# Opening products in another term order, later sample norm, two PSUM tiles for the last product, earlier sample gate

## The chip, the cores and the metric

One Trainium2 chip, one NeuronCore. The metric is the device time of one execution in microseconds (us). Engines are named as in the profile: PE is the matrix engine (PEld its weight loads), DVE the vector engine, ACT the scalar engine, POOL GpSimd, SP the engine that issues most DMAs.

## The reference, cut to what matters

One decoder layer over 1024 prompt rows and 8 sample rows of 1024 channels, all in float32:

```
xn = rmsnorm(h);  proj = xn @ w_in            # 1024 x 7168, split into u, v, z_a, x_b, z_b, g_a, g_b
y_a = gelu(u) * spatial_mix(layernorm(gelu(v))) * silu(z_a)
y_b = pooled(x_b) * silu(z_b)
m = sigmoid(g_a) * (y_a @ w_pa) + sigmoid(g_b) * (y_b @ w_pb)
h = h + rmsnorm(m @ w_out) * post_g
e = p @ w_ple
gate = sigmoid(rmsnorm(h) @ w_pg)
h = h + rmsnorm(gate * e) * ple_out_g
```

The prompt's result and the sample's result are both outputs, with some rows of v and of the pooling input.

## The kernel before, in words

Every large product is cut in seven by Strassen's scheme (P1 to P7), and each factor is split into a high and a low part (`split`, line 432: ACT writes the high part, DVE the difference), so that one product of 512 x 512 blocks is 3 matmuls for each of 4 blocks of the contraction: high x high, high x low, low x high. `product` (line 663) issues these 12 matmuls. The blocks of the normalised input are called B11, B21, B22 and T1 to T4; T1 to T4 are sums of the former that DVE makes in the opening.

No order is written out by hand for the middle of the kernel. The program is first recorded as operations (`Planner.take`, line 211), and a list scheduler (`Planner.order`, line 274) then gives each engine its fixed order by a time model: an operation starts not before its due time minus a lead, among those that could start the one with the earliest due time is taken (`rank`, line 305), and `PUSH` (line 32, through `pushed`, line 989) moves the due time of single kinds of operations: a positive number makes it earlier, a negative one later. All instructions are emitted by `play`, so every row of the profile names L374. At run time each engine works its order off strictly, waiting where an operand is not there. Most tiles live in 46 slots of SBUF that the scheduler hands out; PSUM has three regions of two banks (`region`) and two single banks (`bank`).

Four stages matter here.

- **Opening** (0 to about 70 us). `begin` (line 1726) issues the loads in a fixed order (`WE` and `LOADS` place the weights w_ple and the second v weights among the x tiles). Nine warming matmuls, then products with w_ple (tile `e`), the norm of x, its transposes on PE (`pst`), evacuated by DVE or ACT as `SIDES` says, cuts of B11 and B21, and the first products (tile `acc`). `SCRIPT` orders the rest: ('r', n) is the n-th product, ('n') the norms of the last four x tiles and of the sample, ('x', k) transposes of the second half, ('t') the sums T1 to T4, ('e', q, n) a product with w_ple. The sample's own transposes (`x_extra`, tile `pxe`) end the step 'n'.
- **Output stage** (to 884 us). m times w_out in four pairs of row tiles; 28 products called oflow. The sample's rows get theirs by `sample_steps`, are normalised (`out_finish`, line 1508), get x added by an accumulating DMA from POOL, and are normalised again by `gate_norm` (line 1517, tile `hn`), then transposed on PE (tile `psst`).
- **Gate stage** (884 to 968 us). Again 28 products (gflow, seven for each pair of row tiles) with w_pg. The sample's gate is four rounds of four matmuls of 8 rows (tile `sps`); each round needs two row tiles of the weight (`wgrow`), loaded by SP. `GS` = 12 places loads after gflow[12], [14], [16], [18] and rounds after [14], [16], [18], [20].
- **End.** For row tiles 6 and 7 and the sample, `gate_finish` (line 1572) loads h plainly into a slot (`hback`) and adds it on DVE in halves; for the others an accumulating DMA from POOL adds h. The last pair runs its products in the order `LAST` = P1, P6, P7, P5, P2, P4, P3; P6, P5 and P3 accumulate in one PSUM tile. P3 is issued as two halves of 256 columns (`run_halves`, line 776), each followed by its sigmoid on ACT, both in that one PSUM tile.

## Time and profile before

| what | value |
|---|---|
| median of 3 runs | 978.4 us (977.9 to 978.81) |
| the profiled execution | 978.37 us |
| its span, first to last instruction | 976.7 us |
| PE busy in the span | 963.9 us |
| DVE, ACT, POOL busy | 811.2, 498.4, 72.7 us |
| mean granted PE clock | 0.997 of full speed |

The page gives busy time and instruction count of each engine. The list of waits sums, for an engine, the time that it sat idle and what ended that idle time. A timeline row has the start in us, the duration in us, engine, line, operation, the written tile <- the read tiles, the shapes, how many instructions were merged into the row, and in brackets the idle time just before, with what released the engine. A row of windows gives the busy us of each engine in a stretch.

### The profile page before, as it was taken

What the parts mean: (1) busy time and instruction counts of PE and PEld (TensorE: products, weight loads), DVE (VectorE), ACT (ScalarE), POOL (GpSimd) and SP (SyncE); (2) the same over time, 40 slices, a digit from 0 to 9 for tenths busy, and PEclk for the clock granted to TensorE, in tenths of its full rate; (3) what the DMA queues carried; (4) which work ended last, traced back from release to release, by engine and by line L of the source; (5) the groups of instructions that cost most, each with busy time, mean ns of one, the idle gap of its engine ahead of it and who ended that gap; (6) DMA issues with size and microseconds to landing.
All of it is one profiled execution on the core that took longest, in us unless ns stands there. A gap on an engine that the chain in (4) does not pass through costs nothing. (4 is left out here: it accounts for less than half of the span.)

```text
span 976.7 us, 15913 instructions
## 1 busy us (share of the span) xinstructions
PE 963.9 (99%) x6037; PEld 856.9 (88%) x6037; DVE 811.2 (83%) x1259; ACT 498.4 (51%) x854; POOL 72.7 (7%) x117
## 2 busy tenths in 40 slices
PE   9999999999999999999999999999999999999996
PEld 7889899999999999999999999999999997778775
DVE  6997568978879888868788897688799899779987
ACT  7764446757435443242434343463362273688655
POOL 1200000000000000000010100000000001223212
PEclk9999999999999999999999999999999999999998
DMA  9433955433457464353435376693592494798996
GB/s 328 168 108 77 183 132 195 153 93 126 170 196 269 141 207 162 120 195 119 152 115 184 116 242 233 231 357 102 176 352 88 130 321 153 170 291 296 238 323 197
DMA packets 128506, 185.82 MB, mean 190 GB/s; under 512 B 42150, under 2 KB 85198, under 8 KB 128421
## 3 DMA queue, kind: packets, MB, share of 16 engines
q1 hardware_dynamic: 126381, 177.43, 54.7%
q0 software_dynamic: 2048, 7.37, 4.1%
q8 instruction: 47, 0.77, 0.3%
q14 instruction: 30, 0.25, 0.1%
HBM read 129.27 MB, written 55.96 MB: 190 GB/s over the span
## 5 line engine op out<-in xcount | busy, mean ns | idle before, releaser
L374 DVE TENSOR_TENSOR u<-acc,u 128x520 f32<-128x520 f32 (+1 forms) x89 | 61.9, 696 | 35.2 <-PE acc L374 34.9
L374 POOL TENSOR_TENSOR rstd<-ms,mhalf 128x1 f32<-128x1 f32 (+1 forms) x37 | 29.9, 830 | 517.3 <-DVE ms L374 516.7
L374 ACT ACTIVATE u<-acc 128x512 f32<-128x512 f32 (+1 forms) x43 | 25.6, 595 | 39.8 <-PE acc L374 39.6
L374 DVE TENSOR_TENSOR big<-big 128x1024 f32<-128x1024 f32 (+4 forms) x20 | 24.0, 1218 | 0.1
L374 POOL COPY big<-xb 128x1 f32<-128x1 f32 x8 | 3.4, 425 | 260.2 <-ACT xb L374 219.9
L374 ACT ACTIVATE paw<-pas 128x512 fp32r<-128x512 f32 x16 | 10.0, 629 | 23.6 <-DVE pas L374 18.2
L374 ACT ACTIVATE pbw<-pbs 128x512 fp32r<-128x512 f32 x16 | 10.1, 630 | 22.6 <-DVE pbs L374 17.2
L374 PE MATMUL accm<-qh,wpoolw 128*128 128x260 f32 (+1 forms) x96 | 21.0, 320 | 0.0
L374 ACT ACTIVATE big<-mix 128x256 f32<-128x256 f32 x32 | 12.1, 382 | 16.2 <-PE mix L374 15.5
L374 ACT ACTIVATE gbw<-gbs 128x512 fp32r<-128x512 f32 x16 | 10.1, 629 | 19.9 <-DVE gbs L374 10.6
L374 DVE SCALAR_TENSOR_TENSOR zb<-accm,gvec,zb 128x512 f32<-128x512 f32 (+1 forms) x16 | 12.0, 753 | 9.1 <-PE accm L374 9.0
L374 ACT ACTIVATE zaw<-zas 128x512 fp32r<-128x512 f32 x16 | 10.0, 626 | 17.2 <-DVE zas L374 10.3
L374 ACT ACTIVATE zbw<-zbs 128x512 fp32r<-128x512 f32 x16 | 10.1, 629 | 14.7 <-DVE zbs L374 8.2
L374 ACT ACTIVATE junk<-h 128x512 bf16<-128x512 f32 x25 | 15.7, 627 | 3.5 <-DVE h L374 3.0
L374 PEld LDWEIGHTS accm<-qh,wpoolw 128*128 128x128 f32 x96 | 15.6, 188 | 1.9
L374 ACT ACTIVATE u<-acct 128x512 f32<-128x512 f32 x22 | 13.0, 590 | 7.7 <-PE acct L374 5.3
L374 ACT ACT_TABLE_LOAD x11 | 14.1, 1283 | 5.0 <-PE acc L374 3.4
L374 DVE TENSOR_TENSOR paw<-pas,paw 128x512 fp32r<-128x512 f32 x16 | 10.9, 687 | 6.8 <-ACT paw L374 6.8
L374 ACT ACTIVATE mw<-ms 128x512 fp32r<-128x512 f32 x16 | 10.0, 625 | 12.4 <-DVE ms L374 9.7
L374 ACT ACTIVATE uw<-us 128x512 fp32r<-128x512 f32 x16 | 10.0, 626 | 12.3 <-DVE us L374 10.7
L374 PE MATMUL mix<-wst,vh 128*128 128x256 f32 x64 | 15.5, 320 | 0.0
L374 ACT ACTIVATE zbw<-zbraw 128x512 fp32r<-128x512 f32 x12 | 7.5, 623 | 15.6 <-DMA zbraw<-in_w_in_dram 9.8
(655 smaller groups left out, 3563.7 us busy)
## 6 DMA issues: line engine op xcount, KB each, us to landing
ga<-ga SPq DMA_DIRECT2D x16, 516.0 KB, 5.4
gb<-gb SPq DMA_DIRECT2D x16, 516.0 KB, 6.2
ya<-za SPq DMA_DIRECT2D x8, 516.0 KB, 3.8
yb<-zb SPq DMA_DIRECT2D x8, 516.0 KB, 4.7
x<-in_x_prompt_dram SPq DMA_DIRECT2D x8, 512.0 KB, 7.8
vraw<-in_w_in_dram SPq DMA_DIRECT2D x8, 512.0 KB, 6.9
e<-e SPq DMA_DIRECT2D x8, 512.0 KB, 4.7
vturned<-v SPq DMA_DIRECT2D x32, 128.0 KB, 4.3
```

What stands on the lines that cost most here:

```text
L374: getattr(getattr(self.nc, e), method)(*(self.real(a) for a in args), **{k: self.real(a) for k, a in kwargs.items()})
```

## The change

- `product`: while the plan's clock is under 40 us, the 12 matmuls go in another order: for each half of the contraction first high x high and low (weight) x high (input) of both blocks, then high (weight) x low (input) of both; the scheduler may part them after the 4th, 6th and 10th.
- `x_extra` leaves the step 'n' and stands as step 'y' after 'p'; the transposes of the second half of x follow the fourth product instead of the third; one e product stands one product earlier. One evacuation moves from ACT to DVE (`SIDES`), the second w_ple load goes one x tile earlier, the second v weights two x tiles earlier, and some due times move (`PUSH`).
- `gate_norm` of the sample gets a due time 4 us later.
- The last pair's P6, P5 and P3 accumulate in two PSUM tiles of 256 columns each, one in a region and one in a single bank. P6 and P5 so become 24 matmuls of 256 columns each, and their evacuations two pieces.
- `GS` is 8, and the sample's gate has three rounds: 8, 4 and 4 matmuls after gflow[12], [14] and [16]; the row tiles load after gflow[8], [10], [12], [14].
- Row tiles 4 and 5 are finished as 6 and 7 are: one more multiplication by the gain for each half, a plain load of h, and the addition on DVE in halves, each half stored by itself.

```diff
+ROUNDS = {'wo': (2, 2, 2, 2), 'wg': (4, 2, 2)}
-SIDES = (0, 1, 0, 1, 0, 1, 0, 0)
+SIDES = (0, 1, 0, 0, 0, 1, 0, 0)
-WE = 2
-PUSH = {'norm': -5.0, 'half': 0.0, 'cut': -2.0, 'e': -1.0, 'we': -2.0, 'vw': -5.0, 'p': 3.0}
+WE = 1
+PUSH = {'hs': -4.0, 'norm': -5.0, 'half': 0.0, 'cut': -1.0, 'e': 2.0, 'we': -2.0, 'vw': -9.0, 'p': 3.0}
+BACK = 4
-SCRIPT = (('r', 0), ('n',), ('r', 1), ('p',), ('r', 2), ('x', 0), ('x', 1), ('r', 3), ('b',), ('t',), ('r', 4), ('r', 5), ('e', 2, 0), ...
+SCRIPT = (('r', 0), ('n',), ('r', 1), ('p',), ('y',), ('r', 2), ('r', 3), ('x', 0), ('x', 1), ('b',), ('t',), ('r', 4), ('e', 2, 0), ('r', 5), ...
-LOADS = (('s',), ('x', 4), ('x', 5), ('w', 1), ('x', 6), ('x', 7), ('p',), ('q',))
+LOADS = (('s',), ('w', 1), ('x', 4), ('x', 5), ('x', 6), ('x', 7), ('p',), ('q',))
-OS, GS = 5, 12
+OS, GS = 5, 8
...
     def product(form, ps, weights, operand, what, first, last, again=False):
-        for k in range(4):
-            if k == 2 and plan.clock < EARLY:
+        (wh, wl), early = weights, plan.clock < EARLY
+        terms = [(k, i) for k in range(4) for i in range(3)]
+        if early:
+            terms = [(k, i) for kk in (0, 2) for ii in ((0, 1), (2,)) for k in (kk, kk + 1) for i in ii]
+        for n, (k, i) in enumerate(terms):
+            if early and n in (4, 6, 10):
                 plan.apart()
+            xh, xl = operand.at(what, k)
+            w, x = ((wh, xh), (wl, xh), (wh, xl))[i] if early else ((wh, xh), (wh, xl), (wl, xh))[i]
...
     def strassen_within(weights, operand, user, order=None):
+            if order and p in ("P6", "P5"):
+                for o, c in ps:
+                    if p == "P6":
+                        add(o, o, at["w"][:, c])
+                    nc.scalar.activation(out=at["u" if p == "P6" else "w"][:, c], in_=o, func=AF.Copy)
+                if p == "P5":
+                    user.summed(1, 1, at["r3"], at["w"])
+                return
...
+                if new and order and r == "r2":
+                    two = Tokens.new(), bank("acctb")
+                    at[r] = [(t[:, :QUART], slice(i * QUART, (i + 1) * QUART)) for i, t in enumerate(two)]
...
             def run_halves(a=a, b=b, r=r):
-                for c in (slice(0, QUART), slice(QUART, HALF)):
-                    product(columns(c), at[r], weights.ready[a], operand, b, False, True, True)
-                    user.direct(0, 1, at[r][:, c], slice(HALF + c.start, HALF + c.stop))
+                for o, c in at[r]:
+                    product(Pieces, [(o, c)], weights.ready[a], operand, b, False, True, True)
+                    user.direct(0, 1, o, slice(HALF + c.start, HALF + c.stop))
...
     def sample_steps(key, src, steps, turned, finish):
-        for i, r in enumerate(range(0, NB, 2)):
-            at(steps[2 * i], lambda r=r: load(r))
-            at(steps[2 * i + 2], lambda r=r: run(r))
+        for r in range(0, NB, 2):
+            at(steps[r], lambda r=r: load(r))
+        r = 0
+        for n in ROUNDS[key]:
+            at(steps[r + n], lambda r=r, n=n: run(r, n))
+            r += n
...
-        if t >= NB - 2:
+        if t >= NB - BACK:
             mul(g, g, gains["out"][:r, c])
...
-        if t < NB - 2:
+        if t < NB - BACK:
...
-    at(oflow[OS + 12], lambda: gate_norm(S))
+    at(oflow[OS + 12], lambda: pushed('hs', gate_norm, S))
...
-            x_extra()
```

## Rows read from the trace of the kernel before

**Rows 1.** The page's part 1: busy us (share) and instruction count of each engine.

```profile
PE 963.9 (99%) x6037; PEld 856.9 (88%) x6037; DVE 811.2 (83%) x1259; ACT 498.4 (51%) x854; POOL 72.7 (7%) x117
```

**Rows 2.** List of waits, PE, whole span: us in total, times, longest us.

```profile
PE acct L374 <- ACT h L374: 1.6, 1, 1.6
PE warm L374 <- DVE heat L374: 1.5, 1, 1.5
PE acct L374 <- ACT ge L374: 0.6, 1, 0.6
PE pxe L374 <- DVE xe L374: 0.5, 1, 0.5
```

**Rows 3.** Timeline, PE, 22 to 24 us (columns as told above).

```profile
22.78 0.63 PE L374 MATMUL pxe<-ident,xe 8*128 8x8 f32 x8 [0.47 <-DVE xe L374]
23.34 0.49 PE L374 MATMUL acc<-xB11h,vw 128*128 128x512 f32 x1
```

**Rows 4.** Timeline, DVE, 22 to 27 us.

```profile
22.56 2.34 DVE L374 TENSOR_TENSOR xB11l<-big,xB11h 128x1024 fp32r<-128x1024 f32 x2
24.83 1.39 DVE L374 TENSOR_SCALAR big<-pst,gvec 128x512 f32<-128x512 f32 x2
```

**Rows 5.** Timeline, ACT, 855 to 865 us.

```profile
861.10 1.06 ACT L374 ACTIVATE hn<-hs 8x1024 f32<-8x1024 f32 x1 [2.15 <-DMA hs<-in_x_sample_dram]
...
863.53 0.59 ACT L374 ACTIVATE h<-acct 128x512 f32<-128x512 f32 x1
864.01 1.14 ACT L374 ACTIVATE hn<-hs,rstd 8x1024 f32<-8x1024 f32 x1
```

**Rows 6.** Timeline, PE, 858 to 868 us.

```profile
864.17 0.50 PE L374 MATMUL acct<-woB11h,mw 128*128 128x512 f32 x1 [1.61 <-ACT h L374]
...
867.17 0.66 PE L374 MATMUL psst<-ident,hn 8*128 8x8 f32 x8
```

**Rows 7.** Timeline, PE, 961.6 to 968 us: P4 of the last pair, then P3 in halves.

```profile
961.60 0.40 PE L374 MATMUL acct<-wgT4h,hw 128*128 128x512 f32 x1
...
964.38 0.28 PE L374 MATMUL acct<-wgB22h,hw 128*128 128x256 f32 x1
...
966.06 0.28 PE L374 MATMUL acct<-wgB22h,hw 128*128 128x256 f32 x1
966.90 0.38 PE L374 MATMUL acct<-wgB22h,hw 128*128 128x256 f32 x1 [0.56 <-ACT ge L374]
```

**Rows 8.** Timeline, DVE, 946 to 978 us: additions of h in tiles 7, 6.

```profile
969.64 0.74 DVE L374 SCALAR_TENSOR_TENSOR ge<-ge,rstd,hback 128x512 f32<-128x512 f32 x1
...
970.75 2.07 DVE L374 SCALAR_TENSOR_TENSOR ge<-ge,rstd,hback 128x512 f32<-128x512 f32 x3
```

**Rows 9.** Timeline, PE, 946 to 978 us: one round of the sample's gate.

```profile
946.66 1.04 PE L374 MATMUL sps<-wgrow,sst 128*8 128x512 f32 x8
947.64 0.50 PE L374 MATMUL acct<-wgB11h,hw 128*128 128x512 f32 x1
```

**Rows 10.** Groups by form, PEld, 964.3 to 968.3 us: busy us, mean ns | idle.

```profile
L374 PEld LDWEIGHTS acct<-wgB22h,hw 128*128 128x128 f32 x16 | 2.6, 188 | 0.8 <-ACT ge L374 0.8
```

**Rows 11.** Windows, two stretches: busy us of each engine (instructions), PEclk, DMA share, GB/s.

```profile
50.00:60.00 10.00, 10.00 (x61) 7.96 (x59) 9.93 (x16) 6.82 (x10) 0.00 (x0) 1.00 0.59 196
880.00:890.00 10.00, 10.00 (x45) 8.14 (x44) 10.00 (x12) 9.09 (x17) 0.00 (x0) 1.00 1.04 364
```

**Rows 12.** Timeline, DVE, 48 to 100 us: the last piece of T2's low part.

```profile
57.07 0.26 DVE L374 TENSOR_TENSOR xT2l<-big,xT2h 128x16 fp32r<-128x16 f32 x2
```

**Rows 13.** Timeline, PE, 57.5 to 60.6 us: the first product with T2.

```profile
60.37 0.51 PE L374 MATMUL acc<-xT2h,vw 128*128 128x260 f32 x2
```

**Rows 14.** Timeline, SP, 852 to 978 us: third and fourth row tile's load.

```profile
918.24 1.67 SPq L374 DMA_DIRECT2D wgrow<-wg x2
```

**Rows 15.** Tile wgrow, whole span: how long its loads took to land.

```profile
DMA to landing us min/median/max: 5.8/6.1/10.2
```

**Rows 16.** Timeline, PE, 920.3 to 923.8 us: the product after gflow[12].

```profile
920.80 0.39 PE L374 MATMUL acct<-wgT4h,hw 128*128 128x512 f32 x1
```

More of the change, by code (lines that the diff above doesn't have):

```diff
@@ L642, in hybrid_step @@
         like = staticmethod(lambda t: t)
-    def columns(c):
-        class Part(Tokens):
-            pieces = staticmethod(lambda ps, wide: [(ps[:, c], c)])
-        return Part
+    class Pieces(Tokens):
+        pieces = staticmethod(lambda ps, wide: ps)
     class Turned(Weights):
@@ L666, in product @@
         wide = what not in ("B11", "B21", "T4")
-        for k in range(4):
-            if k == 2 and plan.clock < EARLY:
-                plan.apart()
-            (wh, wl), (xh, xl) = weights, operand.at(what, k)
-            for i, (w, x) in enumerate(((wh, xh), (wh, xl), (wl, xh))):
-                for o, c in form.pieces(ps, wide):
-                    nc.tensor.matmul(o, w[:, k, :], x[:, c],
-                                     start=first and k == 0 and i == 0, stop=last and k == 3 and i == 2,
-                                     skip_group_check=again)
+        (wh, wl), early = weights, plan.clock < EARLY
[4 more added lines that the diff above has]
+            if early and n in (4, 6, 10):
+                plan.apart()
+            xh, xl = operand.at(what, k)
+            w, x = ((wh, xh), (wl, xh), (wh, xl))[i] if early else ((wh, xh), (wh, xl), (wl, xh))[i]
+            for o, c in form.pieces(ps, wide):
+                nc.tensor.matmul(o, w[:, k, :], x[:, c], start=first and n == 0, stop=last and n == 11,
+                                 skip_group_check=again)
     def halves(t, j):
@@ L771, in run @@
                 new = r not in at
-                if new:
+                if new and order and r == "r2":
+                    two = Tokens.new(), bank("acctb")
+                    at[r] = [(t[:, :QUART], slice(i * QUART, (i + 1) * QUART)) for i, t in enumerate(two)]
+                elif new:
                     at[r] = Tokens.new()
+                if order and r == "r2":
+                    product(Pieces, at[r], weights.ready[a], operand, b, new, True, not new)
+                    return
                 product(Tokens, at[r], weights.ready[a], operand, b, new, True, not new)
             def run_halves(a=a, b=b, r=r):
-                for c in (slice(0, QUART), slice(QUART, HALF)):
-                    product(columns(c), at[r], weights.ready[a], operand, b, False, True, True)
-                    user.direct(0, 1, at[r][:, c], slice(HALF + c.start, HALF + c.stop))
+                for o, c in at[r]:
+                    product(Pieces, [(o, c)], weights.ready[a], operand, b, False, True, True)
+                    user.direct(0, 1, o, slice(HALF + c.start, HALF + c.stop))
             if order and p == order[-1]:
@@ L886, in token_matmul, with sample_round @@
                 nc.tensor.matmul(ps, lo(k), wh, start=False, stop=k == w.nk - 1)
-    def sample_round(ps, turned, weights, r):
-        plan.apart()
+    def sample_round(ps, turned, weights, r, apart=True):
+        if apart:
+            plan.apart()
         for q in range(4):
@@ L925, in load, with run @@
                 dma(t, src[k * P : (k + 1) * P, :])
-        def run(r):
+        def run(r, n):
             if not ps:
                 ps.append(bank("sps"))
-            sample_round(ps[0], turned(), lambda k, j: rows[k][:, j * HALF : (j + 1) * HALF], r)
-            if r == NB - 2:
+            lhs = turned()
+            for s in range(r, r + n, 2):
+                sample_round(ps[0], lhs, lambda k, j: rows[k][:, j * HALF : (j + 1) * HALF], s, s == r)
+            if r + n == NB:
                 finish(ps[0])
-        for i, r in enumerate(range(0, NB, 2)):
-            at(steps[2 * i], lambda r=r: load(r))
-            at(steps[2 * i + 2], lambda r=r: run(r))
+        for r in range(0, NB, 2):
[4 more added lines that the diff above has]
+            r += n
     roots = {}
@@ L1805, in begin @@
               "b": lambda: xop.cut("B22"), "e": lambda q, n: embed_both(q, n), "t": combines, "m": small_tables,
-              "s": embed_sample_last}
+              "s": embed_sample_last, "y": x_extra}
         prepared[0] = 1
```

2 lines of the change are left out of this document (1 added, 1 removed).

## The prediction, made before the changed kernel was run

> **What bounds the kernel now.** I read the page's busy times first: PE works 963.9 us of a span of 976.7, so 12.8 us are idle, and nothing but PE's own work or those 12.8 us can be won [rows 1]. The next view is the list of waits of PE, which says where the idle time is: 1.5 us at the start, before the first warming matmul, 0.5 us in the opening, 1.6 us near the end of the output stage and 0.6 us in the last product, 4.2 us together [rows 2]. The other 8.6 us are the tail, the evacuation, norm and store behind the last matmul. The timelines then show what stands behind each wait; they are taken up below. DVE is the second engine to watch: over the whole span it is busy 83% [rows 1], but in the opening and at the change from output to gate stage it is full, 9.93 and 10.00 us of 10 [rows 11]. So an earlier PE is an earlier end only where DVE can follow.
>
> The profiled execution took 978.37 us, 1.7 us more than its span, and agrees with the median of 978.4, so the sum is made against either. About 0.2%, 2.0 us, is what a measurement of this kernel can tell from no change; faster and slower below mean beyond 976.4 and 980.4.
>
> **The opening.** PE idles 0.47 us until DVE has scaled the sample's x (`xe`), only to run the sample's eight small transposes, and then starts the first product at 23.34 [rows 3]. With `x_extra` two steps later those transposes still cost PE their time, but the 0.47 us before them goes, if the high part of B11 is there. The second part of the gain is the order of terms: B11's low part is two DVE instructions of together 2.34 us from 22.56, so its first half is ready about 23.73, while the old order wants it as the second matmul, 0.23 us after 23.34; the wait that this makes, about 0.2 us, is below what the list of waits names. High parts first want it four matmuls, 0.93 us, after the start [rows 3, 4]. I take 0.7 us off. The ends are 0 (the vector engine's other work fills the gap) and 1.2 (the small bubbles around it go too). The price is one evacuation of two 512-column pieces that goes from ACT to DVE: 1.39 us for such a pair on DVE [rows 4], in a stretch where DVE is full [rows 11]. What is late next is T2: its last low piece ends at 57.33 and the first product with it starts at 60.37, so DVE has 3.0 us of slack there [rows 12, 13]. Of those, 1.4 go to the evacuation and 0.7 to the earlier PE, and 0.9 stay. So I cost the evacuation at nothing, with up to 0.7 us if that cover is gone. The moved loads cost nothing by themselves: SP issues the same ones, and the x tiles that come later have their transposes later too.
>
> **The sample's norm.** PE waits 1.61 us for ACT's copy of a PSUM tile into `h`, which ends at 864.12 [rows 5, 6]. ACT is late because it works in order: ahead of that copy stands the square of the sample's row (`hn`), for which ACT sat idle 2.15 us until POOL's accumulating DMA had landed, and then 1.06 us of work [rows 5]. The due time 4 us later lets the scheduler place the copy ahead of it. Then the copy ends about 3.2 us sooner, before PE asks for the tile at 862.56, and the whole 1.61 us goes. What comes later is the sample's own chain: the scaling of `hn` ends at 865.15 and PE transposes the result at 867.17, 2.0 us after it [rows 5, 6], and the rounds that use it are 50 us away [rows 16]. PE would wait there only if the chain slips by more than those 2.0 us and the transposes keep their place. I take 1.6 off, with the ends 0 and 1.6.
>
> **Sample's gate.** A round holds PE 0.98 us, from its first matmul to the next large product [rows 9]. Eight matmuls in one go do the same array work and leave out one change between the 8-row and the full products. The trace shows no double round; the saving lies between 0 and 0.3, I take 0.2. The larger effect is off PE: about nine DVE instructions of 512 columns, some 0.7 us each by the 0.74 of one such addition [rows 8], and as many on ACT, leave the last 15 us of the kernel for the stretch around 935 us.
>
> **Last product and end.** Twelve of P3's 24 matmuls of 256 columns make the first half, but fifteen start, from 964.38 to 966.06, 0.12 us apart; then PE waits for ACT, and the sixteenth starts at 966.90 [rows 7]. So 0.84 - 0.12 = 0.72 us are lost because both halves are one tile. With two tiles nothing joins them, and 0.72 goes. P6 and P5 as 24 matmuls each cost a little: a full-width product is 12 matmuls in 2.78 us (961.60 to 964.38), 0.232 each, against 0.24 for two narrow ones [rows 7], so 24 x 0.008 = 0.2 us on PE. Their evacuations in halves have another product's 2.8 us as cover.
>
> Not all of the 0.72 arrives at the end, because DVE then has four additions of h in a row, the first at 969.64, the last three 2.07 us from 970.75 [rows 8]. The first pair (tile 7) hangs on P4, not on P3. If tile 7's chain stays, only 0.2 arrives; if DVE, free of the sample, runs it some tenths sooner, up to 0.9. I take 0.6. Tiles 4 and 5 add four multiplications on DVE, 4 x 0.7 = 2.8 us, against the sample's 6.3 that left, and take two accumulating DMAs off POOL; both lie beside the last pair's products and I cost them at nothing, with 0.3 us as the other end if they push tile 7's chain.
>
> **Sum:** 978.4 - 0.7 - 1.6 - 0.2 + 0.2 - 0.6 = 975.5 us.
>
> **A rule that speaks against the split.** P3's 256-column matmuls, each with a weight load of its own of 188 ns, start 0.12 us apart [rows 7, 10], so the loads overlap the matmuls. The Trainium skill, "TensorE: Matmul & The Clock Gate", section "Part 3: Packing small matmuls", says that weight loads overlap running matmuls only when their row groups differ, which full 128-row weights' do not. By that rule P5's and P6's 24 further loads would stand bare on PE. The trace contradicts it.
>
> **The rivals.**
> 1. The 1.6 us stays or comes back. Either the copy still stands behind the sample's square, or PE arrives earlier at a gate stage whose DVE is full (10.00 of 10) [rows 11] and waits there for an evacuation or a weight's low part instead. For it: DVE can't follow faster than its own work. Against: DVE's and ACT's chains were held by the same square and move forward with it. Time 975.5 + 1.6 = 977.1.
> 2. The opening's gain is given back at T2, when DVE's shift is over the 0.9 us that I left: 976.2. For it: DVE 9.93 of 10; against: the 3.0 us of slack.
> 3. Slower: the earlier double round meets its weights too late. It needs four row tiles of the weight after gflow[12], at 920.80 [rows 16]. Before, the third and fourth were issued from 918.24 to 919.91 [rows 14], landing 6.1 us later in the median and 10.2 at most [rows 15]: 926.0 at the median. PE works in order, so if those issues stay where they were, PE waits 5.2 us, and the time is 975.5 + 5.2 = 980.7. It decides as soon as the fourth load is issued later than about 914.7. For it: SP is in order too, slots are scarce, and two more row tiles at once need two more of them. Against: the loads' due times move with the rounds.
> 4. More than I count goes: the opening's 1.2 and the end's 0.9: 978.4 - 1.2 - 1.6 - 0.9 = 974.7.
> 5. The bare weight loads: 24 x 188 ns = 4.5 us [rows 10], 980.0. By the 0.12 us of rows 7 it has 1 in 100.
>
> **How the numbers follow.** Forecast 975.5: 0.47. Rival 1: 0.19. Rival 2: 0.12. Rival 3: 0.13. Rival 4: 0.08. Rival 5: 0.01. Some 0.05 of the forecast's own spread lies above 976.4. So faster is 0.47 + 0.12 + 0.08 - 0.05 = 0.62, same 0.19 + 0.05 + 0.01 = 0.25, slower 0.13. The range leaves out rival 3: its lower end, 973.9, is rival 4 with 0.3 for the double round, nothing for P5 and P6, and the 0.5 us by which the lowest of the three runs lies below the median (974.7 - 0.3 - 0.5); its upper end, 978.2, is rival 1 with the opening at 0 and the end at 0.2 (977.1 + 0.7 + 0.4).
>
> **What would show it.** In the changed trace PE's waits for `xe`, for ACT's `h` and for ACT's `ge` should be gone from the list, and the first `acc` matmul should start about 0.7 us sooner, near 22.6. The copy into `h` should stand ahead of the first `hn` row on ACT. The `sps` rows should be three, the first of sixteen entries, with no bracket on them; a bracket naming the DMA of `wgrow` is rival 3. A bracket at the first `xT2h` row is rival 2, and a new wait for DVE or ACT between 866 and 915 us is rival 1. P3 should start 24 matmuls 0.12 us apart. The prediction is wrong if the list of waits holds a new entry of over 1 us, or if the tail, 8.6 us now, grows.

## The result and the profile after

The changed kernel takes 981.24 us (median of 18 runs, 978.88 to 982.65), the kernel before 978.27 in the same comparison (18 runs, 976.69 to 979.6). The ratio is 1.0022, with a 95% interval of 1.0015 to 1.0029, so it is 1.5 to 2.8 us slower by the ratio and 3.0 by the medians, where 975.5 and "faster" were forecast. The profiled execution of the changed kernel was the slowest of the 18, 982.65 us with a span of 980.9. So single numbers of its trace are up to 1.4 us later than usual, and the table under "The experiments" sets it beside others.

The page's first part of the changed kernel answers [rows 1]. PE has 0.8 us more of work, DVE 4.3 us more:

```profile
PE 964.7 (98%) x6061; PEld 856.9 (87%) x6061; DVE 815.5 (83%) x1268; ACT 498.6 (51%) x854; POOL 71.0 (7%) x115
```

The list of waits of PE answers [rows 2]. The waits for `xe`, for ACT's `h` and for ACT's `ge` are gone, as forecast. The one for `heat` stays, and others are new:

```profile
PE acct L376 <- ACT u L376: 2.0, 3, 1.4
PE vecs L376 <- DMA vecs<-in_ple_in_g_dram: 1.6, 1, 1.6
PE warm L376 <- DVE heat L376: 1.5, 1, 1.5
PE pst L376 <- DVE big L376: 0.7, 1, 0.7
PE acc L376 <- DVE big L376: 0.3, 1, 0.3
```

The wait for `vecs` belongs to this execution: the kernel all_swap, told of below, has the same opening, and there it is 0.0 us; in all traces it lies between 0.0 and 1.6.

**The opening.** The timelines of PE, then of DVE, of the changed kernel, where [rows 3, 4] stood:

```profile
36.15 2.78 PE L376 MATMUL pst<-ident,x 128*128 128x128 f32 x24
39.65 1.06 PE L376 MATMUL pst<-ident,x 128*128 128x128 f32 x8 [0.72 <-DVE big L376]
40.97 1.17 PE L376 MATMUL acc<-xB11h,vw 128*128 128x512 f32 x4 [0.25 <-DVE big L376]
```

```profile
35.88 1.41 DVE L376 TENSOR_SCALAR x<-x,rstd 128x1024 f32<-128x1024 f32 x2
37.20 0.68 DVE L376 TENSOR_TENSOR vs<-vraw 128x512 f32<-128x512 f32 x1
38.10 4.07 DVE L376 TENSOR_SCALAR big<-pst,gvec 128x512 f32<-128x512 f32 x6 [0.21 <-PE pst L376]
```

The first product starts at 23.13, 0.2 us sooner than before in a trace that is 1.2 us behind at 19 us. The sample's eight transposes run at 30.83 and wait for nothing now. But the second half's x are scaled only by 37.3, its transposes start at 36.15 (in before at 31.56, most of them at 33.38), and six evictions of them come in one row of 4.07 us. PE waits behind them twice.

**Change from output to gate stage.** The timelines of ACT, DVE and PE, where [rows 5] and [rows 6] stood:

```profile
862.62 0.57 ACT L376 ACTIVATE h<-acct 128x512 f32<-128x512 f32 x1
...
871.93 1.06 ACT L376 ACTIVATE wgB11h<-wgB 128x1024 fp32r<-128x1024 f32 x1 [1.28 <-DVE big L376]
...
873.70 0.60 ACT L376 ACTIVATE u<-acct 128x512 f32<-128x512 f32 x1 [0.20 <-DVE acct L376]
```

```profile
870.65 1.25 DVE L376 STREAM_TRANSPOSE big<-hblocks 128x1024 f32<-128x1024 f32 x1 [1.98 <-DMA hblocks<-h]
...
872.98 0.69 DVE L376 TENSOR_TENSOR acct<-acct,u 128x512 f32<-128x512 f32 x1
```

```profile
874.35 0.50 PE L376 MATMUL acct<-woT1h,mw 128*128 128x512 f32 x1 [1.44 <-ACT u L376]
```

The copy into `h` ends at 863.2, and PE does not wait for it. Then DVE waits 1.98 us for the blocks of h, in order, and behind its transposition stand the sum `acct`, ACT's copy `u` and PE's product woT1, which starts at 874.35 after 1.4 us.

**The rounds.** PE, where [rows 9] stood:

```profile
925.75 1.90 PE L376 MATMUL sps<-wgrow,sst 128*8 128x512 f32 x16
927.58 0.50 PE L376 MATMUL acct<-wgB11h,hw 128*128 128x512 f32 x1
...
930.56 2.02 PE L376 MATMUL sps<-wgrow,sst 128*8 128x512 f32 x8
932.51 0.50 PE L376 MATMUL acct<-wgT2h,hw 128*128 128x512 f32 x1
```

The double round holds PE 1.83 us, two single ones would hold it 1.96. The second round holds it 1.95 instead of 0.98: in PEld's list of waits there is one of 0.9 us for the DMA of `wgrow`. The third round runs at 947.04; the last of before ran at 946.66 [rows 9]. By the order of the products on PE it stands behind 20 of them, where the change has it behind 17 (gflow[16]) and before had its last behind 21. Its weights were issued at 933.96 and 935.25, in before at 933.33 and 934.29. So the sample's gate is sooner by one product instead of four; why the order puts it there the rows do not show.

**The end.** Busy time by stretch (columns as in [rows 11]), of before and then of the changed kernel:

```profile
964.00:968.00 4.00, 3.44 (x27) 3.15 (x25) 3.49 (x8) 1.95 (x5) 0.00 (x0) 1.00 1.02 339
968.00:972.00 4.00, 0.23 (x2) 0.03 (x1) 3.96 (x10) 1.38 (x5) 1.59 (x2) 0.95 0.74 295
972.00:976.00 4.00, 0.00 (x0) 0.00 (x0) 0.83 (x2) 0.00 (x0) 0.00 (x0) 0.50 0.53 197
```

```profile
964.00:968.00 4.00, 3.87 (x17) 2.85 (x16) 3.91 (x7) 2.03 (x5) 0.97 (x2) 1.00 0.85 311
968.00:972.00 4.00, 3.13 (x26) 2.88 (x24) 4.00 (x10) 2.46 (x6) 0.00 (x0) 1.00 0.58 213
972.00:976.00 4.00, 0.00 (x0) 0.00 (x0) 4.00 (x12) 1.56 (x6) 1.52 (x2) 0.78 0.01 2
```

DVE (third pair of numbers) was already full behind the last matmul in before, 3.96 of 4. Now it is full for 12 us on end, 11.91. The additions of h on DVE, where [rows 8] stood:

```profile
965.85 0.75 DVE L376 SCALAR_TENSOR_TENSOR ge<-ge,rstd,hback 128x512 f32<-128x512 f32 x1
...
967.73 1.41 DVE L376 SCALAR_TENSOR_TENSOR ge<-ge,rstd,hback 128x512 f32<-128x512 f32 x2
...
969.71 0.74 DVE L376 SCALAR_TENSOR_TENSOR ge<-ge,rstd,hback 128x512 f32<-128x512 f32 x1
...
974.54 2.74 DVE L376 SCALAR_TENSOR_TENSOR ge<-ge,rstd,hback 128x512 f32<-128x512 f32 x4
```

The first four belong to tiles 4 and 5 and stand ahead of tiles 6 and 7, which hang on the last products. The sample's last two passes stand before them:

```profile
961.46 1.40 DVE L376 SCALAR_TENSOR_TENSOR ge<-ge,rstd,hback 8x512 f32<-8x512 f32 x2
```

They end at 962.86, in before they ended at 964.58: some 2 us sooner, and far from the stretch around 935. P3, where [rows 7] stood, now runs through; the first and the last of its 24 matmuls on PE, then the loads of its high weights, by tile:

```profile
968.12 0.28 PE L376 MATMUL acct<-wgB22h,hw 128*128 128x256 f32 x1
...
970.86 0.28 PE L376 MATMUL acctb<-wgB22h,hw 128*128 128x256 f32 x1
```

```profile
L376 PEld LDWEIGHTS acctb<-wgB22h,hw 128*128 128x128 f32 x8 | 1.3, 189 | 0.0
L376 PEld LDWEIGHTS acct<-wgB22h,hw 128*128 128x128 f32 x7 | 1.1, 188 | 0.0
```

The last matmul ends at 971.13, the span 9.8 us later. In before it was 8.4.

### The profile page after: what moved, and what is told of

The parts are those of the page before. It is cut to its first block, busy times and chain, and to the rows that moved or that the text cites. A ratio compares the mean times of both kernels' runs of the same rounds, so it can differ in the third digit from the quotient of the medians.

```text
span 980.9 us, 15982 instructions
## 1 busy us (share of the span) xinstructions
PE 964.7 (98%) x6061; PEld 856.9 (87%) x6061; DVE 815.5 (83%) x1268; ACT 498.6 (51%) x854; POOL 71.0 (7%) x115
## 5 line engine op out<-in xcount | busy, mean ns | idle before, releaser
L376 ACT ACTIVATE u<-acct 128x512 f32<-128x512 f32 (+1 forms) x22 | 12.5, 570 | 9.6 <-DVE acct L376 5.5
L376 ACT ACTIVATE gbw<-gbraw 128x512 fp32r<-128x512 f32 x12 | 7.4, 624 | 16.2 <-DMA gbraw<-in_w_in_dram 14.1
L376 PE MATMUL mix<-wst,vh 128*128 128x256 f32 x64 | 15.5, 320 | 0.0
```

The lines of the kernel that those rows point to most:

```text
L376: getattr(getattr(self.nc, e), method)(*(self.real(a) for a in args), **{k: self.real(a) for k, a in kwargs.items()})
```

## The experiments

Every kernel was timed beside the kernel before on the same chip; before took 978.40 to 978.61 in these comparisons and 978.27 in that of after. The ratio's column is a 95% interval. The table is worked out from the traces. The middle columns are what PE lost (+) or gained (-) against the trace of before in one stage: the start of the same product in both, and the difference's growth over the stage. The last two are from the last matmul's end to the last store's issue on SP, and from there to the end of the span. A single trace carries the luck of its execution: in the kernels that leave opening and norm alone, the stage from 819 to 864 differs by -1.28 to +0.61 us, and at 19 us, ahead of the table, the traces are 0.2 to 1.2 us behind before's. So what counts is what all kernels with a part share. Each edit also gives the scheduler another program to order, so a part alone is the part and its new order.

```
kernel     median  ratio to before    19-49 49-819 819-864 864-912 912-956 956-end | to store, to end
before     978.4                                                                   |  4.62  3.82
o_open     978.24  0.9988 to 1.0007   +0.58  -0.64  -1.00   +1.08   -0.01   +0.01  |  4.62  3.39
open_act   979.34  0.9996 to 1.0019   +0.49  -0.68  -1.75   +2.22   +0.04   -0.04  |  4.62  3.94
o_hs       978.24  0.9985 to 1.0007   -0.01  +0.02  -1.77   +1.94   +0.01   -0.03  |  4.62  3.83
hs_swap    979.35  1.0005 to 1.0026   +0.01  +0.01  -1.23   +6.09   -0.06   -0.02  |  4.62  3.81
firsts     979.08  0.9992 to 1.0010   +0.57  -0.63  -1.72   +1.59   +0.16   -0.01  |  4.62  3.39
no_sg      979.05  0.9996 to 1.0014   +0.02  +0.56  -0.15   -0.03   +0.01   -0.04  |  4.62  3.46
o_back     978.83  0.9994 to 1.0012   -0.01  -0.03  +0.61   +0.46   +0.02   +0.01  |  5.28  3.19
o_two      980.10  1.0008 to 1.0026    0.00  +0.01  -1.05    0.00   +0.06   -0.12  |  6.12  4.75
o_gs       981.17  1.0016 to 1.0034    0.00  +0.01  -1.09   -0.02   +1.95   +0.13  |  4.89  4.77
gs_double  981.16  1.0017 to 1.0035   +0.02  -0.01  -0.76   -0.03   +0.49   -0.87  |  7.45  4.59
gs_early   982.88  1.0035 to 1.0060   +0.01  +0.37  -1.28   +0.97   +0.01   +0.26  |  6.77  4.89
ends       980.21  1.0008 to 1.0026    0.00  +0.12  -0.43   -0.03   +1.43   -0.39  |  6.20  3.18
u_two      980.89  1.0015 to 1.0036   +0.56  -0.63  -1.72   +1.14   +0.81   +0.87  |  5.55  3.62
u_back     980.93  1.0017 to 1.0038   +0.57  -0.63  -1.72   +0.73   +1.00   -0.48  |  5.34  4.42
u_gs       979.86  1.0006 to 1.0023   +0.57  -0.63  -1.72   +1.34   +0.05   -0.77  |  6.68  3.43
after      981.24  1.0015 to 1.0029   +0.58  -0.55  -1.72   +2.59   +1.18   -0.34  |  6.17  3.62
all_swap   981.08  1.0020 to 1.0044   +0.58  -0.60  -1.63   +1.72   +0.70   -0.37  |  6.21  3.62
```

### One part alone

The change was cut into five: the opening (order of terms, SCRIPT, SIDES, WE, PUSH, LOADS), the norm (`PUSH['hs']`), the gate (ROUNDS, GS), the two tiles (`Pieces`, `acctb`) and tiles 4 and 5 (BACK). Each was put alone into before. The opening:

```diff
-SIDES = (0, 1, 0, 1, 0, 1, 0, 0)
+SIDES = (0, 1, 0, 0, 0, 1, 0, 0)
-WE = 2
+WE = 1
...
+            w, x = ((wh, xh), (wl, xh), (wh, xl))[i] if early else ((wh, xh), (wh, xl), (wl, xh))[i]
```

> The kernel before with the opening's part alone: term order, later transposes of the sample, moved evacuation, loads and due times. Theory A (the opening as changed costs time: a new wait for the three small gain vectors of 1.6 us and new waits at the transposes of the second half of x of 1.1 us, against 0.5 us for xe that goes): 979.5 us, 1.2 over before. Rival B (the wait for the vectors is the luck of one execution, the rest balances): 978.3 us, within 0.4 of before. My first forecast had 977.6.

The norm:

```diff
-    at(oflow[OS + 12], lambda: gate_norm(S))
+    at(oflow[OS + 12], lambda: pushed('hs', gate_norm, S))
```

> The kernel before with the sample's norm 4 us later and nothing else. Theory A (the wait of 1.6 us for ACT's copy into h goes, but PE waits about 1.4 us a few products later, where DVE's transposition stands waiting for its blocks ahead of P6's evacuation): 978.1 us, 0.2 under before, with an entry acct <- ACT u over 1 us in the list of PE's waits. Rival B (that later wait belongs to other parts of the change; the 1.6 us is won): 976.7 us.

The gate:

```diff
-OS, GS = 5, 12
+OS, GS = 5, 8
+ROUNDS = {'wo': (2, 2, 2, 2), 'wg': (4, 2, 2)}
```

> The kernel before with the sample's gate four products sooner in three rounds and nothing else. Theory A (the rounds meet their weights late and the slots and DMAs they take delay others): 979.2 us, 0.9 over before, with a wait of PE or its weight loads for the DMA of wgrow. Rival B (DVE and ACT freed at the end shorten the tail): 977.5 us.

The two PSUM tiles:

```diff
+                    two = Tokens.new(), bank("acctb")
+                    at[r] = [(t[:, :QUART], slice(i * QUART, (i + 1) * QUART)) for i, t in enumerate(two)]
```

> The kernel before with the last pair's P6, P5 and P3 in two PSUM tiles and nothing else. Theory A (0.72 us of PE's time goes, 0.2 comes for the narrow matmuls, and all of it reaches the end): 977.8 us, 0.5 under before. Rival B (DVE's additions at the end are the bound, only the place of the wait changes): 978.3 us, the time from the last matmul to the end 0.5 us longer.

The opening and the norm, 978.24 each against 978.47, bring nothing that can be measured; the opening's forecast of 0.7 us lies inside its interval, the norm's of 1.6 just outside. In o_hs the wait for `u`, where theory A wanted over 1 us, is 0.77:

```profile
872.84 0.50 PE L376 MATMUL acct<-woT1h,mw 128*128 128x512 f32 x1 [0.77 <-ACT u L376]
```

The gate costs 2.7 us, the two tiles 1.6, both more than either of their theories allowed. Put into before, tiles 4 and 5 gave:

```diff
-BACK = 2
+BACK = 4
```

> Tiles 4 and 5 by plain loads alone, beside before's everything else. VectorE gets two passes by the gain and two additions for each tile in place of one pass of 1.24 us, some 1.3 us more per tile, of which before's VectorE has some room between 940 and 958 (13.0 of 18 us busy) and none behind 958. Theory A (VectorE full at the end decides): the last additions come 0.5 to 2.5 us later, 979.0 to 980.5. Theory B (the stores behind the accumulating DMAs decide): before's own stores of those tiles wait for landings at 962.8 and 967.4 and nothing stands behind them too late, so nothing is gained or lost: 978.0 to 978.7.

978.83 against 978.61, not to be told from no change, between the two theories: the stretch from the last matmul to the last store grows by 0.66 us, from 4.62 to 5.28, and the rest, to the end, shrinks by 0.63, from 3.82 to 3.19.

What the gate does in its trace: DVE, then PE, of o_gs.

```profile
933.38 1.25 DVE L376 STREAM_TRANSPOSE big<-hblocks 128x1024 f32<-128x1024 f32 x1 [2.80 <-DMA hblocks<-h]
934.54 0.67 DVE L376 TENSOR_TENSOR acct<-acct,u 128x512 f32<-128x512 f32 x1
...
960.53 1.28 DVE L376 SCALAR_TENSOR_TENSOR ge<-ge,rstd,out 128x1024 f32<-128x1024 f32 x1 [0.54 <-POOL rstd L376]
...
962.34 1.27 DVE L376 SCALAR_TENSOR_TENSOR ge<-ge,rstd,out 128x1024 f32<-128x1024 f32 x1
```

```profile
935.90 0.50 PE L376 MATMUL acct<-wgT1h,hw 128*128 128x512 f32 x1 [0.37 <-ACT u L376]
```

Six of the eight loads of `wgrow` now stand on SP ahead of a set of loads of h's blocks, whose second load, issued at 916.64, lands at 932.12. DVE waits 2.80 us for the blocks, the sum behind them is late, and PE waits 0.37 us at 935.90 and 0.38 at 957.18; the second round waits 1.0 us for its weights. Together they make most of the stage's +1.95. At the end the sample's passes stand ahead of the scaling of tiles 4 and 5 (960.53 and 962.34 above; 2.46 us from 955.26 in before). Their accumulating DMAs then go out 5 us before the last matmul ends instead of 10, and the last stores take 4.77 us to the end instead of 3.82. The five of the table's kernels that issue the last such DMA less than 6 us ahead of that end (o_two, o_gs, gs_double, gs_early, u_back) need 4.4 to 4.9 us there, all others 3.2 to 3.9. In SP's list of waits behind 955 us, of before and then of o_gs, the wait for such a DMA grows:

```profile
SPq L374 <- DMA ge<-h: 2.3, 1, 2.3
```

```profile
SPq L376 <- DMA ge<-h: 7.7, 1, 7.7
```

In o_two the fourth round came one product later, at 949.20 instead of 946.66, and with it the sample's passes. DVE then ran on with one pause, of 0.18 us:

```profile
958.33 0.68 DVE L376 TENSOR_TENSOR ge<-eback,ge 8x512 f32<-8x512 f32 x1 [0.31 <-ACT ge L376]
958.94 2.46 DVE L376 SCALAR_TENSOR_TENSOR ge<-ge,rstd,out 128x1024 f32<-128x1024 f32 x2
...
971.04 2.73 DVE L376 SCALAR_TENSOR_TENSOR ge<-ge,rstd,hback 128x512 f32<-128x512 f32 x4
```

The last matmul ended 0.29 us sooner than in before, at 967.94, and the last store was issued 1.2 us later. So the split does what it says on PE, and DVE keeps the gain and more. Whether the two tiles themselves or the later round they brought with them cost the 1.6 us, no run separates.

### One part taken away

Without tiles 4 and 5's plain loads:

> The change without one part: tiles 4 and 5 get h again by the accumulating DMA (two passes of 1.24 us on VectorE and one DMA per tile), everything else as in the kernel after. Theory A, VectorE is the bound of the end (busy 11.91 of the last 12 us from 964 to 976 in the kernel after, 8.28 before): each of the two tiles costs VectorE two passes by the gain and two additions, 4 x 0.63 = 2.5 us, in place of 1.24; taken away, about 2.5 us leave VectorE's queue behind 960, and as before's stretch from the last matmul to the end was 8.4 us against 9.76 now, up to 1.3 us come back: 979.3 to 980.2 where the kernel after shows 981.2. Theory B, the stores on SyncE's queue are the bound (in gs alone the store of tile 5 waited for the accumulating DMA's landing at 971.0 and pushed the last four stores): the accumulating DMAs return and the end stays as late, 981.0 or more. Theory C, the loss sits on TensorE ahead of the last product: nothing of it changes, 981.2.

Without the gate:

> The change without one part: the sample's gate in four rounds, from the 12th step, as before. Theory A (VectorE full at the end): in the kernel after the third round ran at 947.0, as late as the fourth before (946.7), so the sample's passes reach VectorE no earlier by the change; without the double round TensorE saves the 0.9 us that its loads waited for the late rows of weights, but VectorE's queue of the end is no shorter: 980.3 to 981.2. Theory C (the loss is on TensorE): the whole that gs cost alone, 2.7 us (981.17 against 978.47), comes back, 978.5.

Without the two tiles:

> The change without one part: the last pair's second product in one PSUM tile, 128x512, as before. Theory A: two tiles alone cost 1.6 us by VectorE running without a pause from 958 to 972, with four additions of 0.68 us left after the last matmul instead of three; without it 979.6 to 980.4, the saving smaller than 1.6 because tiles 4 and 5 still fill VectorE. Theory C: P3's nine waits of some 0.03 to 0.1 us return, and P4 has ACT's 0.5 us back on TensorE: 981.2 to 981.9.

Without the opening and the norm:

> The three parts of the end together (sample's gate in three rounds, two PSUM tiles, tiles 4 and 5 by plain loads), with the opening and the place of the sample's norm as before. The opening alone (978.24) and the norm alone (978.24) moved nothing against 978.47. If they move nothing beside the other three either, this kernel takes what the kernel after takes, 981.2 (980.9 to 981.7). If what they gain on TensorE early (1.6 us at 840, by the trace of the opening alone) is worth something that the full end hides, it takes 982.0 or more; if the two are themselves a loss beside the others (their early gain lets work crowd), 980.5 or less.

Of the three parts of the end only the gate's removal gives something back by the medians, 1.4 us (979.86 against 981.24), half of what the gate costs alone; the intervals overlap (1.0006 to 1.0023, 1.0015 to 1.0029). It lies between what A and C expect, as does u_two. The time of u_back is nearest to B and C, but its trace shows A and B each at work: the stretch to the last store shrinks by 0.83 us (6.17 to 5.34) and that from there to the end grows by 0.80 (3.62 to 4.42), so the two ways of bringing h to tiles 4 and 5 cost the same here. `ends` is 1.0 us better than the whole, as if the opening and the norm cost something beside the rest; again the intervals overlap. C alone cannot be the answer: in all ten kernels of the table that have the gate or the two tiles, the way from the last matmul to the end is longer than before's 8.44 us, by 0.7 to 3.6. In the seven that have neither it is 8.0 to 8.6.

The two first parts together:

> The opening and the later place of the sample's norm together, the end as before. Alone each took 978.24 against 978.47. If their gains on TensorE (1.6 us at 840 by the opening; 1.6 at 864 by the norm) are given back later by waits whatever comes before, because VectorE's transposition at 870 waits for the landing of h's blocks: 977.8 to 978.5. If the gains only cancel by chance in each, the two together reach the 2.3 us that was forecast for them: 976.1. If together they do what they do in the kernel after (a 1.4 us wait for ScalarE's u at 874): 978.5 to 979.5.

979.08 against 978.61, a ratio of 0.9992 to 1.0010: the second of the three falls, the 2.3 us do not arrive. The number lies in the third's range, but its wait of 1.4 us is not there: PE waits 0.45 us for `u` at 873.29 and 0.38 at 893.44. So the gains are given back, in smaller pieces than either of the others had it.

### The two halves of the gate, and what it could bring

The double round, with GS at 12:

```diff
+ROUNDS = {'wo': (2, 2, 2, 2), 'wg': (4, 2, 2)}
```

> One half of the part on the sample's gate alone, beside before's everything else: its first two rounds run as one, but its weights are loaded at the same steps as before (the first round two steps later than before, the last where it was). Theory D, what cost 2.7 us in the whole part alone is that the loads of the weights were moved ahead of the transposing loads of h on SyncE's queue: here they are not, so VectorE's wait for those loads stays near before's 1.3 us (3.4 in the whole part alone), the products that wait for ScalarE's u stay at none, and the time is 978.2 to 979.0. Theory E, the double round itself (2.06 us against twice 0.97, and what queues behind it) costs: 980 to 981.

The sooner steps, with four rounds:

```diff
-OS, GS = 5, 12
+OS, GS = 5, 8
```

> The other half alone: four separate rounds, as before, but loads and rounds four steps sooner, so the last round falls where it fell in the whole part. Theory D: the loads pass the transposing loads of h as they do in the whole part, VectorE waits 2.5 us or more in one stretch for them near 930, and TensorE some 0.4 us for ScalarE's u behind it, twice; the last stores wait again for the accumulating DMAs: 980.5 to 981.5. Theory E: without the double round nothing is lost: 978.0 to 979.0.

981.16 and 982.88 against 978.61: both lose, 2.6 and 4.3 us, more than any of the ranges, so neither D nor E is the whole. In gs_early the loads did pass the blocks, as D has it: DVE waits 5.4 us for them in four waits, 2.9 the longest. In gs_double DVE's wait for the blocks is 1.6 and PE's waits are small, as D has it too; its 2.6 us are all at the end, 7.45 us to the last store. There the last round ran at 949.80, as in o_two and u_gs (949.20 and 949.80). Those three need the longest to the last store among the kernels whose loads kept their place: 6.1 to 7.5 us.

```diff
     sample_sums(ps, o)
     for j in range(2):
-        gated(S, half(j), o[:NS, half(j)])
-    gate_finish(S)
+        dma(y_of(S)[:, half(j)], o[:NS, half(j)])
```

> Before with the sample's gate left out behind its two sums: no sigmoid, product, norm, gain or addition of h for the sample's eight rows, whose output is the bare sums. It shows the most that a sooner gate could bring. By before's trace these passes take VectorE some 4.6 us between 958 and 965, and behind them VectorE still waits 0.51 us for ScalarE at 967.9, with the last matmul at 968.2: nothing of them stands on the path that ends, so 978.0 to 978.6 (theory J, there was nothing to gain by a sooner gate). Rival K (the passes hold up the last additions): 2 us or more less, 976.5 or below.

979.05 against 978.53, a ratio of 0.9996 to 1.0014: nothing is won, as theory J has it. With the sample's passes gone DVE stands idle 1.59, 0.79 and 0.68 us between 959 and 964, and the last store still comes 4.62 us after the last matmul, to the hundredth as in before. So in before a sooner gate could not have brought anything. In the kernel after, where DVE is full to the end, the passes were not left out.

### What takes the opening's gain back

```diff
-SIDES = (0, 1, 0, 0, 0, 1, 0, 0)
+SIDES = (0, 1, 0, 0, 0, 1, 0, 1)
```

> The opening alone, with one eviction of the second half (its last pair of PSUM tiles) on ScalarE instead of VectorE. In the opening alone TensorE gained 1.54 us between 19 and 30 us and lost 2.1 by 49, where the transpositions waited 0.89 and the first product behind them 0.42 for VectorE, which evicted six tiles in a row, 4.07 us. Theory H (VectorE's row of evictions is what gives the gain back): the row is four tiles, 2.7 us, the two waits go, the stage from 19 to 49 us gains 0.5 or more where it lost 0.57, and the time is 977.0 to 977.8. Rival I (the transpositions start late, because the half's x are scaled late, and any split waits): the waits stay above 0.8 in sum and the time is 978.0 to 978.6.

DVE, then PE, of open_act:

```profile
35.83 1.41 DVE L376 TENSOR_SCALAR x<-x,rstd 128x1024 f32<-128x1024 f32 x2
...
38.05 2.73 DVE L376 TENSOR_SCALAR big<-pst,gvec 128x512 f32<-128x512 f32 x4 [0.21 <-PE pst L376]
```

```profile
39.61 1.07 PE L376 MATMUL pst<-ident,x 128*128 128x128 f32 x8 [0.72 <-DVE big L376]
40.92 1.17 PE L376 MATMUL acc<-xB11h,vw 128*128 128x512 f32 x4 [0.25 <-DVE big L376]
```

979.34 against 978.53, a ratio of 0.9996 to 1.0019 and above both ranges. The row is four evictions long instead of six, and the two waits are the same to the hundredth. Theory H falls, and the waits are as rival I has them: what is late is the start of the evictions. Its reason is not borne out. DVE does scale the second half's x until 37.2, where before had done so by 33.0, but at the row's start it waits 0.21 us for PE's transposes, and those wait for nothing: the order puts them behind the fourth product, where PE, busy without a bracket, comes to them at 36.10.

### What takes the norm's gain back

```diff
-            op.lands = 2.0
+            op.lands = 12.0 if name.startswith('hblocks') else 2.0
```

> The sample's norm later, alone, with one thing more: the planner counts 12 us for the landing of the loads that bring h's blocks (2 us otherwise), so it lists VectorE's transposition of those blocks behind the addition acct + u of the third product, where it stood ahead of it. With the norm later alone, TensorE gained 1.72 us at 864 and lost 1.94 by 912 in three waits for ScalarE's u, behind VectorE's wait of 2.5 us for the blocks at 869. Theory F (the in-order wait for the blocks hands the gain back): those waits for u are gone, TensorE is still some 0.8 us or more ahead at 912, and the time is 0.5 to 1.0 below the control with 12 us and the norm where it was. Rival G (something else, such as the sample's work itself, holds the third product): the waits for u stay at 0.8 us or more in sum, and the two kernels take the same.

> The control: before with the 12 us alone, the sample's norm where it was. TensorE keeps its wait for ScalarE's copy into h near 862 (0.5 to 2.4 us in the profiles without the norm's part, the middle one 0.8), and has no wait for u. Otherwise as before, 978.0 to 979.0; if the order of the gate stage suffers by the larger allowance, more.

987.14 and 986.28 us against 978.53 (neither is in the table): the allowance reordered the whole gate stage, so the pair can't answer its question. It shows what the order alone is worth here: nearly 8 us from one constant of the planner.

The other way was to exchange two instructions in the finished order, in the norm alone and in the kernel after. In the edit `at` is the fourth transposition of blocks of h, `acc` the next sum into `acct`, `u` ACT's copy of that sum and `hw` its copy of what was transposed:

```diff
-        return [(e, call) for _, _, e, call in sorted(calls, key=lambda c: c[:2])]
+        made = [(e, call) for _, _, e, call in sorted(calls, key=lambda c: c[:2])]
...
+        part = [c for i, c in enumerate(made[at : u + 1], at) if i not in (at, hw)]
+        where = next(i for i, c in enumerate(part) if c is made[acc]) + 1
+        return made[:at] + part[:where] + [made[at]] + part[where:] + [made[hw]] + made[u + 1 :]
```

> The sample's norm later, alone, with two instructions exchanged in the finished order and nothing else: VectorE's transposition of the blocks of h near 869 stands behind the addition acct + u of the third product instead of three places ahead of it, and ScalarE's copy hw, which reads it, behind ScalarE's copy u. (The larger allowance changed the whole order and told nothing.) Theory F, the in-order wait of 2.5 us for the blocks is what hands the norm's gain back: the wait of 0.93 us for u near 872 goes, VectorE's idle time there falls by more than 1 us, the waits of 0.60 at 892 and 0.27 at 912 shrink, and the time is 977.2 to 977.8. Rival L, VectorE's own work bounds the pairs behind it (busy back to back from 883 to 896 in the norm's part alone): the wait at 872 goes, but what TensorE is ahead it loses again at 892 and 912, and the time is 978.0 to 978.6, as without the exchange.

> The kernel after with the same exchange of two instructions. It had a wait of 1.4 us for u at 874 and further ones of 0.53, 0.24, 0.38 and 0.30 behind it. Theory F: the first is gone and with it 0.8 to 1.4 us of the time: 979.8 to 980.4. Rival L: 0.5 us or less comes through, 980.7 to 981.3, because the end is set by VectorE's passes behind 958.

979.35 against 978.40, above both ranges, and 981.08, in rival L's: no gain. But in hs_swap the exchange did not take the wait for `u` away, so it does not decide on theory F there. DVE, then ACT, of hs_swap:

```profile
870.55 0.70 DVE L386 TENSOR_TENSOR acct<-acct,u 128x512 f32<-128x512 f32 x1 [0.71 <-PE acct L386]
871.16 1.24 DVE L386 STREAM_TRANSPOSE big<-hblocks 128x1024 f32<-128x1024 f32 x1
```

```profile
872.43 1.06 ACT L386 ACTIVATE wgB11h<-wgB 128x1024 fp32r<-128x1024 f32 x1 [2.44 <-DVE big L386]
873.39 0.58 ACT L386 ACTIVATE u<-acct 128x512 f32<-128x512 f32 x1
```

The sum is now ready at 871.25, but ACT copies it only at 873.39: ahead of `u` stands ACT's cut of the gate's weights, which waits until DVE's transposition is done, and PE's gap ahead of woT1, worked out from the matmuls' starts, is 0.96 us where it was 0.93. That cut does not read `big`; that it waits for the buffer which the transposition frees is argued, not shown. In o_hs the same cut waits 1.84 us for DVE's `big` at 870.41. In all_swap the wait shrinks from 1.44 to 0.80 us, PE is 0.9 us better off by 912, and the time is 0.2 better, which can't be told from nothing. Behind it, from 883 to 896 in o_hs, DVE is busy but for 0.11 us, as rival L has it, and PE waits for `u` 0.60 us at 892 and 0.27 at 912 (from the starts; 0.43 and 0.10 by the brackets). So the in-order wait for the blocks is one holder of the product, the cut on ACT another, and how much each hands back stays open. The traced execution of hs_swap, 984.03 us, is one of four of its twelve between 982 and 984; there a load of weights issued at 867.13 landed 15 us later.

## Why the prediction was wrong

**The sum's terms.** *Opening, -0.7.* PE gained 1.54 us between 19 and 30 us in the opening alone, 0.56 of it the transposes that run later. By 49 us it was 0.58 behind. That is rival 2 in its effect, at another place: I looked for the next late thing at T2 [rows 12, 13], and it was the second half's transposes, 20 us earlier, which the change itself moved behind the fourth product. DVE's 9.93 of 10 us [rows 11] is read there from 50 us on; the stretch of the scaling and the transposes, 28 to 42 us, I didn't read. Between 49 and 819 us 0.55 to 0.68 come back in every kernel with the opening, in small steps; what that is the rows do not show.

*Norm, -1.6.* The mechanism was right: no kernel with the part alone or beside others, hs_swap excepted, shows the wait of [rows 6]. The size was that of one execution. In the nine other traces without the part (the one with the larger allowance left out) the same wait was 0.0 to 2.2 us, 0.6 in the median, because it hangs on when POOL's DMA lands [rows 5]. And the gain is lost again, 0.7 to 2.6 us by 912 in the seven traces with the part beside hs_swap's: rival 1, which I gave 0.19. The two traces with the opening alone, without the norm, lose 1.1 and 2.2 there too, so the loss is not the norm's only. Its condition, DVE 10.00 of 10 between 880 and 890 us [rows 11], stood in the text and was the better evidence.

*Double round, -0.2.* It saves 0.13 us (1.83 against 1.96). Rival 3 put its wait at the first round and at 5.2 us; it came at the second round, 0.4 to 1.2 us in the six kernels with the rounds moved and joined. The loads did move, and part of the price was paid by the loads of h's blocks behind them on SP, which no rival named.

*Last product, -0.6.* On PE it came as worked out: in the kernel after P3 runs its 24 matmuls 0.12 us apart from 968.12 to 970.86, without a wait. This also settles rival 5: the loads take 188 ns each on PEld, and none stands bare on PE. The sentence of the Trainium skill, "TensorE: Matmul & The Clock Gate", section "Part 3: Packing small matmuls", that weight loads overlap running matmuls only when their row groups differ, does not hold in these traces. But nothing arrives at the end: in o_two and in the kernel after, DVE is full there.

**The step that failed.** The sum has two halves, and each was run by itself. The first half took two waits of PE, 0.7 and 1.6 us, off the end in full ("the whole 1.61 us goes", "I take 1.6 off"). In `firsts` the two together bring nothing: 979.08 against 978.61, at best 0.8 us by the interval where 2.3 were forecast. The waits go, but PE loses 2.1 us between 30 and 49 us and 1.6 between 864 and 912. The text said that an earlier PE is an earlier end only where DVE can follow, and the sum did not keep to it.

The second half, -0.2 + 0.2 - 0.6, measured +1.7 us in `ends` (980.21 against 978.50; +0.8 to +2.5 by the interval). The step there is "The larger effect is off PE": the sample's passes were to leave the last 15 us for the stretch around 935. The last round came one product sooner instead of four, the passes end at 962.86 instead of 964.58, and in before there was nothing to gain from it (no_sg). That relief was set against the passes of tiles 4 and 5 ("I cost them at nothing"), and no row was read for DVE's room at the end: the windows of before show it 3.49 and 3.96 us busy of 4 from 964 to 972. Tiles 4 and 5 did lengthen the stretch to the last store, by 0.66 us in before and by 0.83 in after, but the stores behind them took 0.63 and 0.80 less, so that at nothing they came out about right, by luck. The cost lies with the gate, where 0.2 us was to be won and 2.7 are lost alone and, by the medians, 1.4 beside the others, and with the two tiles, 1.6 alone and, not to be told from nothing, 0.4 beside the others. Those shares do not add up, and how the 1.7 us divide stays open.

The two halves do add up: 0.5 and 1.7 us by the medians, where the whole is 2.2 by the ratio and 3.0 by the medians. Of the tail the text said that the prediction is wrong if it grows; it grew from 8.44 to 9.79 us. The rest is PE's: in the table's row of after +3.77 us between 864 and 956, less the 1.72 won before and the 0.34 behind.

## What to carry to other kernels

Where an order is planned ahead and each engine works it off in order, an edit's price is the new order, not its instructions: read who stands behind each moved load and each moved pass on every engine. Before work is moved to the end or taken from it, look at the second engine's busy time in the last windows, and leave the work out once to see whether it matters at all. A wait that hangs on a DMA's landing is sized from several executions, not from one.

## What was not expected of the hardware

Loads of the same tile landed 3 us after their issue or 15: h's blocks 3.4 us in before (911.15 to 914.58) and 15.5 in o_gs (916.64 to 932.12), where six loads of weights were issued in the 6 us ahead of them. A tile of weights took 15.0 in hs_swap, `wgrow` 5.8 in after. That the loads ahead make the difference is argued, not shown. And 18 executions of the changed kernel spread over 3.8 us, of before over 2.9, with a granted clock of 0.997 in both traces.
